# Rotary embedding moved from the retention blocks to the gate projection, and the last MLP's products reordered, in a two-block transformer kernel

## Chip, cores and metric

One core of a Trainium2 chip runs the whole program. The metric is the device time of one execution in microseconds: the kernel before has a median of 2659.2 us over 3 runs (2658.93 to 2669.19).

## What is computed

Two transformer blocks in float32, on 1024 tokens of 1024 features (cut to what the change touches):

```python
# block 1, token mixer: half of the width is retention, half gated linear attention (gla)
rq, rk, rv, rg, gq, gk, gv, gg, glr = split(u @ w_in)
q, k = rotary(rq), rotary(rk)          # [x1*cos - x2*sin, x2*cos + x1*sin] on each head of 128
ro = head_norm(retention(q, k, rv)) * silu(rg)
go = head_norm(gla(gq, gk, gv, log_a)) * silu(gg)
m  = concat(ro, go) @ w_out
# ... block 1's MLP, then block 2: mixer, cross attention, and at the end
h = layer_norm(ALPHA * h + relu(h @ w1)**2 @ w2)   # block 2's MLP: the output
```

## The kernel before

Every large product is made of three float32r matmuls (`mm3`, L114 to L116: high times high, high times low, low times high), so each operand is split into a high and a low page: ScalarE casts (L82), VectorE subtracts (L83). Pages of 128x1024 come from fixed pools: 8 each for W, H and X, 6 for S (staging), 6 of the smaller `half`. Loads are issued by SyncE in one queue. The program is written as Python generators that are woven; a scheduler with its own model then fixes one order of instructions for each engine, and each engine and each queue keeps to its order.

**The stretch around the rotary embedding.** `ret_proj` makes 24 tiles of 24 matmuls: first 8 token tiles of the gate `rg` (`tok_proj`: tanh on ScalarE, one VectorE product at L436, a store to DRAM), then 16 tiles of q and k by feature, which ScalarE copies out and stores in the DRAM tensor `r_qk`. For every 10 of these tiles about 3 steps of the 8 gla blocks are woven in (`gla_block`, three steps each; L544 are its score matmuls, L552 the VectorE copies that take them out of PSUM, L478 its last transposes). What is left of the gla blocks runs after the last tile. The gate's weights fill all 8 W pages; q and k are projected in four groups of 4 W pages. `ret_setup` loads the value weights `r_W` (8 W pages). Then 8 `ret_block`s follow in a pipe. Each loads its 128 columns of `r_qk` (L623), the same with the two halves of each head exchanged (L624, L625), and the cosines and sines (L626); GpSimd multiplies by the cosine (L631), VectorE by the sine (L632), VectorE adds (L633). In between TensorE projects the block's values (24 matmuls, L627). After L633 come the scores (L637) and the transposes of k (L642), the masking (L638, and L639 on GpSimd), the outputs (L648, L649), the state (L651, L654) and the head norm, which ends in transposes (L478, behind a GpSimd product, L475).

**The end.** `mlp` multiplies the hidden pages by the second weights in Strassen's form: seven half-size products, in groups of two over 8 chunks (`P[0]` in one half of PSUM, `P[1]` in the other), the last one, `T4`, alone:

```python
for g, prods in enumerate((((0, "B11"), (3, "T1")), ((4, "T2"), (5, "T3")), ((1, "B21"), (6, "B22")))):
    P = [banks(True), banks(False)]
...
P = banks(True)          # T4: rows 4 to 7
```

`T4` completes output tiles 4 to 7; tiles 0 to 3 are complete after the third group and are normalized and stored while `T4` runs. The last two chunks of `T4` are done tile by tile, so that each tile's normalization can start: subtract (L1023), statistics (L155), a chain of small VectorE instructions, the scaling (`normalize`: L171 on ScalarE for tiles below 4, else L173 on VectorE), the affine step (L1047, L1048) and the store.

Of the kernel before, what the change touches and what calls it, by code (L numbers as in the profile page):

```python
# [368 lines left out]
class Mix1(Net):  # L369
# [219 lines left out]

    def ret_proj(self, T):  # L590
        nc, I = self.nc, self.I
        self.r_gd = yield from self.tok_proj(T, 1536, "rg", True)
        self.r_qk = self.dram([128, 2, 4, S], "r_qk")
        for s in range(2):
            for g in range(2):
                W = self.wcols(I["w_in"], 512 * s + 256 * g, 256)
                for m in range(2):
                    for h in range(2):
                        ps = self.feat_out(T, W, slice(128 * m, 128 * m + 128), h)
                        o = self.ev()  # L600
                        nc.scalar.copy(out=o, in_=ps)
                        nc.scalar.dma_start(out=self.r_qk[:, s, 2 * g + m, 512 * h:512 * h + 512], in_=o)
                        yield

    def ret_setup(self):
        nc, I = self.nc, self.I
# [9 lines left out]
    def ret_block(self, i, T):  # L616
        nc = self.nc
        sl = slice(128 * i, 128 * i + 128)
        qk = self.page("H").rearrange("p (s h c) -> p s h c", s=2, c=128)
        sw = self.page("H").rearrange("p (s h c) -> p s h c", s=2, c=128)  # L620
        cs = self.half([128, 2, 128])
        vg = self.page("H")
        nc.sync.dma_start(out=qk, in_=self.r_qk[:, :, :, sl])  # L623
        nc.sync.dma_start(out=sw[0:64], in_=self.r_qk[64:128, :, :, sl])  # L624
        nc.sync.dma_start(out=sw[64:128], in_=self.r_qk[0:64, :, :, sl])  # L625
        nc.sync.dma_start(out=cs, in_=self.I["k_rot"][:, :, sl])  # L626
        nc.scalar.copy(out=vg[:, 0:512], in_=self.tok_out(T, self.r_W, i))  # L627
        nc.sync.dma_start(out=vg[:, 512:1024], in_=_rows(self.r_gd, i))
        v8 = lambda z: z.rearrange("p s h c -> p (s h) c")
        b8 = lambda z: cs[:, z].unsqueeze(1).broadcast_to([128, 8, 128])  # L630
        nc.gpsimd.tensor_tensor(out=v8(qk), in0=v8(qk), in1=b8(0), op=ALU.mult)  # L631
        nc.vector.tensor_tensor(out=v8(sw), in0=v8(sw), in1=b8(1), op=ALU.mult)  # L632
        nc.vector.tensor_tensor(out=qk, in0=qk, in1=sw, op=ALU.add)  # L633
        A, kT = sw[:, 0], sw[:, 1]
        ps = self.ps("tr").rearrange("p (h c) -> p h c", c=128)
        for h in range(4):
            nc.tensor.matmul(out=ps[:, h, :], lhsT=qk[:, 1, h, :], rhs=qk[:, 0, h, :], start=True, stop=True)  # L637
        nc.vector.tensor_tensor(out=A, in0=ps, in1=self.r_tab[:, 0], op=ALU.mult)  # L638
        nc.gpsimd.tensor_tensor(out=qk[:, 0], in0=qk[:, 0], in1=self.r_tab[:, 1], op=ALU.mult)  # L639
        ps = self.ps("tr").rearrange("p (h c) -> p h c", c=128)  # L640
        for h in range(4):
            nc.tensor.transpose(ps[:, h, :], qk[:, 1, h, :], self.ident)  # L642
# [13 lines left out]
        yield from self.head_norm(o[:, 0], vg[:, 512:1024], self.norm_w[:, 0:4], True, A, kT)  # L656
        nc.sync.dma_start(out=self.r_od[:, :, sl], in_=kT)
# [64 lines left out]
    def mlp(self, T, w1, w2, res, last, gate=None, then=None, end=None, aff=None):  # L722
# [249 lines left out]

        if gate is not None:
            gate = gate()
        for g, prods in enumerate((((0, "B11"), (3, "T1")), ((4, "T2"), (5, "T3")), ((1, "B21"), (6, "B22")))):
            P = [banks(True), banks(False)]
            for c in range(NC):
                if g == 0:
# [17 lines left out]
            for t in range(4):  # L996
                if g == 0:
                    nc.scalar.copy(out=R(t + 4), in_=P[1][t])
                elif g == 1:
                    tt(out=L(t + 4), in0=P[1][t], in1=R(t), op=ALU.add)  # L1000
                    tt(out=R(t), in0=R(t), in1=R(t + 4), op=ALU.add)
                    tt(out=R(t + 4), in0=R(t + 4), in1=L(t + 4), op=ALU.add)
                else:
                    tt(out=R(t), in0=P[1][t], in1=R(t), op=ALU.add)
        P = banks(True)
        tail = []
        for c in range(NC):
# [63 lines left out]
class Mix2(Mix1):  # L1071
# [714 lines left out]
    def block2_mlp(self, T):  # L1786
# [1 line left out]
        ln3 = self.affine(I["ln3_g_2"][0], I["ln3_b_2"][0])  # L1788

        def last(t, y, st):  # L1790
            self.normalize(y, y, t < 4, st)
            ln3(y)
            self.nc.sync.dma_start(out=_rows(self.O, t), in_=y)

# [145 lines left out]
```

## Time and profile before

| | |
|---|---|
| median of 3 runs | 2659.2 us |
| the profiled execution | 2663.38 us |
| its span, first to last instruction | 2661.6 us |
| mean granted TensorE clock | 0.978 |
| TensorE, VectorE busy | 2549.6 us (96%), 1886.3 us (71%) |
| ScalarE, GpSimd busy | 1170.3 us (44%), 240.3 us (9%) |

Around the span lie 1.8 us of the execution. Busy shares are means over stages with different limits; the stretch from 300 to 614 us (projections, gla and retention blocks) and the last 30 us are to be read by themselves.

### The profile page before, as it was taken

Reading aid. Unit: us, or ns where it says so; the run is one execution under the profiler, and the core shown is the slowest. Engines: PE = TensorE matmul, PEld = TensorE weight load, DVE = VectorE, ACT = ScalarE, POOL = GpSimd, SP = SyncE. Lnnn points to the kernel's source line nnn. Section 1 sums busy time; section 2 is a strip of 40 time slices with the busy share of each in tenths; the row PEclk is TensorE's granted clock in tenths of the full one; section 3 lists DMA queues with packets and bytes.
Section 4 is the critical chain, followed back from the end, with each engine's and each line's share of the span. In section 5 each row is a group of like instructions: output and inputs, shape, how many; then the busy total and the mean of one; then the engine's idle time right before and its main releaser. Section 6 shows DMA issues by size and latency. Waiting matters only on the chain. (4 is left out here: it accounts for less than half of the span.)

```text
span 2661.6 us, 33023 instructions
## 1 busy us (share of the span) xinstructions
PE 2549.6 (96%) x12086; PEld 2069.9 (78%) x12086; DVE 1886.3 (71%) x3205; ACT 1170.3 (44%) x1863; POOL 240.3 (9%) x222
## 2 busy tenths in 40 slices
PE   7899999889999999999999998999998999999997
PEld 7586777678888888888877776778876888888885
DVE  5858666688897777656965577785568777777759
ACT  3622233344654444433543574552237444444332
POOL 4121135540000000000000002100000000000000
PEclk8899999999999999999999999999998999999998
DMA  9772433464175668857632243361102755799763
GB/s 338 245 258 99 146 99 101 147 173 141 72 246 204 217 239 315 298 181 242 198 137 76 69 142 115 119 225 49 40 32 104 252 202 186 270 335 333 267 225 143
DMA packets 255130, 484.36 MB, mean 182 GB/s; under 512 B 21604, under 2 KB 110964, under 8 KB 254968
## 3 DMA queue, kind: packets, MB, share of 16 engines
q1 hardware_dynamic: 247768, 470.59, 51.4%
q10 hardware_dynamic: 7200, 11.67, 1.2%
q8 instruction: 95, 1.56, 0.2%
q14 instruction: 67, 0.55, 0.1%
HBM read 338.80 MB, written 143.38 MB: 181 GB/s over the span
## 5 line engine op out<-in xcount | busy, mean ns | idle before, releaser
L114 PE MATMUL ps<-U,W 128*128 128x512 f32 (+1 forms) x1080 | 427.4, 396 | 10.3 <-ACT ev L776 5.1
L114 PE MATMUL ps<-W,H 128*128 128x512 f32 x1088 | 425.2, 391 | 3.6 <-DVE sm L167 3.0
L83 DVE TENSOR_TENSOR W<-S,W 128x1024 fp32r<-128x1024 f32 (+1 forms) x272 | 333.4, 1229 | 132.5 <-ACT W L82 131.4
L115 PE MATMUL ps<-U,W 128*128 128x512 f32 (+1 forms) x1080 | 425.6, 394 | 1.5 <-DVE U L341 1.5
L115 PE MATMUL ps<-W,H 128*128 128x512 f32 x1088 | 424.5, 390 | 0.0
L116 PE MATMUL ps<-W,H 128*128 128x512 f32 x1088 | 424.4, 390 | 0.0
L116 PE MATMUL ps<-U,W 128*128 128x512 f32 (+1 forms) x1080 | 423.6, 392 | 0.8 <-DVE W L83 0.8
L82 ACT CAST W<-S 128x1024 fp32r<-128x1024 f32 x288 | 298.6, 1043 | 250.2 <-PE ps L115 167.9
L82 ACT CAST H<-S 128x1024 fp32r<-128x1024 f32 x130 | 136.5, 1050 | 292.0 <-PE ps L115 214.9
L83 DVE TENSOR_TENSOR H<-S,H 128x1024 fp32r<-128x1024 f32 x130 | 158.7, 1221 | 144.7 <-ACT H L82 139.9
L114 PEld LDWEIGHTS ps<-U,W 128*128 128x128 f32 (+1 forms) x1080 | 201.2, 186 | 60.7 <-ACT ev L776 5.4
L114 PEld LDWEIGHTS ps<-W,H 128*128 128x128 f32 x1088 | 204.8, 188 | 47.2 <-DVE X L1023 4.1
L115 PEld LDWEIGHTS ps<-U,W 128*128 128x128 f32 (+1 forms) x1080 | 201.3, 186 | 49.7 <-DVE U L341 4.6
L116 PEld LDWEIGHTS ps<-U,W 128*128 128x128 f32 (+1 forms) x1080 | 201.2, 186 | 46.6 <-DVE W L83 1.9
L116 PEld LDWEIGHTS ps<-W,H 128*128 128x128 f32 x1088 | 204.6, 188 | 42.2
L115 PEld LDWEIGHTS ps<-W,H 128*128 128x128 f32 x1088 | 204.8, 188 | 41.9
L116 PE MATMUL ps<-W,U 128*128 128x512 f32 x352 | 140.0, 398 | 5.4 <-DVE U L83 5.4
L114 PE MATMUL ps<-W,U 128*128 128x512 f32 x352 | 142.0, 403 | 1.2 <-DVE X L274 0.8
L115 PE MATMUL ps<-W,U 128*128 128x512 f32 x352 | 140.6, 399 | 0.4 <-DVE W L83 0.4
L776 ACT ACTIVATE ev<-ev 128x512 f32<-128x512 f32 x104 | 65.5, 630 | 140.0 <-DVE ev L874 116.6
L116 PEld LDWEIGHTS ps<-W,U 128*128 128x128 f32 x352 | 67.2, 191 | 20.6 <-DVE U L83 6.7
L777 ACT ACTIVATE X<-ev 128x512 f32<-128x512 f32 x128 | 81.0, 635 | 3.5
(527 smaller groups left out, 4521.2 us busy)
## 6 DMA issues: line engine op xcount, KB each, us to landing
S<-mlp_h SPq DMA_DIRECT2D x112, 512.0 KB, 5.0
S<-in_w_ff SPq DMA_DIRECT2D x96, 512.0 KB, 5.0
mlp_h<-X SPq DMA_DIRECT2D x96, 512.0 KB, 4.4
S<-in_mlp_w SPq DMA_DIRECT2D x96, 512.0 KB, 4.6
mlp_w<-S SPq DMA_DIRECT2D x96, 256.0 KB, 2.7
S<-mlp_w SPq DMA_DIRECT2D x48, 512.0 KB, 4.7
S<-in_w_in SPq DMA_DIRECT2D x46, 512.0 KB, 5.2
X<-in_w_ada SPq DMA_DIRECT2D x32, 512.0 KB, 6.7
```

The lines of the kernel that those rows point to most:

```text
L82: self.nc.scalar.copy(out=hi, in_=src)
L83: (lo_eng or self.nc.vector).tensor_tensor(out=lo, in0=src, in1=hi.bitcast(F32), op=ALU.subtract)
L114: mm(out=ps, lhsT=lh, rhs=rh, start=start and k == 0, stop=False)
L115: mm(out=ps, lhsT=lh, rhs=rl, start=False, stop=False)
L116: mm(out=ps, lhsT=ll, rhs=rh, start=False, stop=stop and k == n - 1)
L776: nc.scalar.activation(out=r, in_=x, func=ACTF.Relu)
L777: nc.scalar.activation(out=out, in_=r, func=ACTF.Square)
```

## The change

1. `ret_proj` projects q and k first, then the gate. After each gate tile it calls the new `rotate(i)`: the four loads of before, three VectorE products and sums (the cosine product too, which was GpSimd's), and a store of the result to a new DRAM tensor `r_rot`.
2. `ret_block` loads its columns from `r_rot`: one load in place of four, and no rotary arithmetic.
3. In the MLP of block 2 alone (`then is None`), `T4` runs third and the group of `B21` and `B22` last. So tiles 4 to 7 are completed early, and the tail, its last two chunks tile by tile, completes tiles 0 to 3 with two products each. `last` normalizes on ScalarE except for tile 3.

```diff
     def ret_proj(self, T):
         nc, I = self.nc, self.I
-        self.r_gd = yield from self.tok_proj(T, 1536, "rg", True)
         self.r_qk = self.dram([128, 2, 4, S], "r_qk")
+        self.r_rot = self.dram([128, 2, 4, S], "r_rot")
...
+        rg = self.tok_proj(T, 1536, "rg", True)
+        for i in range(NB):
+            next(rg)
+            self.rotate(i)
+            yield
...
+    def rotate(self, i):
...
+        nc.sync.dma_start(out=qk, in_=self.r_qk[:, :, :, sl])
+        nc.sync.dma_start(out=sw[0:64], in_=self.r_qk[64:128, :, :, sl])
+        nc.sync.dma_start(out=sw[64:128], in_=self.r_qk[0:64, :, :, sl])
+        nc.sync.dma_start(out=cs, in_=self.I["k_rot"][:, :, sl])
...
+        nc.vector.tensor_tensor(out=v8(qk), in0=v8(qk), in1=b8(0), op=ALU.mult)
+        nc.vector.tensor_tensor(out=v8(sw), in0=v8(sw), in1=b8(1), op=ALU.mult)
+        nc.vector.tensor_tensor(out=qk, in0=qk, in1=sw, op=ALU.add)
+        nc.sync.dma_start(out=self.r_rot[:, :, :, sl], in_=qk)
...
-        nc.sync.dma_start(out=qk, in_=self.r_qk[:, :, :, sl])
-        nc.sync.dma_start(out=sw[0:64], in_=self.r_qk[64:128, :, :, sl])
-        nc.sync.dma_start(out=sw[64:128], in_=self.r_qk[0:64, :, :, sl])
-        nc.sync.dma_start(out=cs, in_=self.I["k_rot"][:, :, sl])
+        nc.sync.dma_start(out=qk, in_=self.r_rot[:, :, :, sl])
...
-        nc.gpsimd.tensor_tensor(out=v8(qk), in0=v8(qk), in1=b8(0), op=ALU.mult)
-        nc.vector.tensor_tensor(out=v8(sw), in0=v8(sw), in1=b8(1), op=ALU.mult)
-        nc.vector.tensor_tensor(out=qk, in0=qk, in1=sw, op=ALU.add)
...
+        if then is None:
+
+            P = banks(True)
+            for c in range(NC):
+                (Hp, Wp), = operands(c, ((2, "T4"),))
+                product(P, c, Hp, Wp)
+                if c % 2:
+                    add_rest(4 + c // 2)
+            for t in range(4):
+                tt(out=L(t + 4), in0=L(t + 4), in1=P[t], op=ALU.subtract)
+            P = [banks(False), banks(True)]
+            tail = []
+            for c in range(NC):
+                ops = operands(c, groups[2])
+                if c >= NC - 2:
+                    tail.append((c, ops))
+                    continue
...
+                if c < 4:
+                    last(c + 4, y[c + 4], None)
+                    add_rest(c)
+            for t in range(4):
+                for c, ops in tail:
+                    for z, (Hp, Wp) in enumerate(ops):
+                        product(P[z], c, Hp, Wp, tiles=(t,))
+                tt(out=L(t), in0=P[0][t], in1=L(t), op=ALU.add)
+                tt(out=R(t), in0=P[1][t], in1=R(t), op=ALU.add)
+                last(t, y[t], None)
+            return
...
-            self.normalize(y, y, t < 4, st)
+            self.normalize(y, y, t != 3, st)
```

What this does to the order of two engines, at three places. Line numbers of the changed program are its own: L627 to L629 are the rotary instructions, L655 the scores of a retention block, L1096 and L1097 the affine step of the output (L1047 and L1048 before), L1050 and L1051 the last additions of the left and the right half of a tile.

VectorE where the value weights `r_W` are split (L83, W from S), before; the last gla blocks' copies out of PSUM (L549, L552) and factors (L536) stand around:

```order
L536 TENSOR_TENSOR X_4033<-X_4023,H_4020 128x896
L536 TENSOR_TENSOR X_4072<-X_4062,H_4020 128x896
L83 TENSOR_TENSOR W_4259<-S_4257,W_4258 128x1024
L83 TENSOR_TENSOR W_4265<-S_4263,W_4264 128x1024
L549 TENSOR_TENSOR half_3875<-ps_3889,ident 128x256
L552 COPY_PREDICATED half_3875<-half_2298,ps_3889 128x256 x3
L552 COPY_PREDICATED half_3875<-half_2298,ps_3902 128x256 x2
L83 TENSOR_TENSOR X_4273<-S_4271,X_4272 128x1024
L552 COPY_PREDICATED half_3875<-half_2298,ps_3902 128x256
```

The same place in the changed program (sm and rs are the small instructions of gla block 4's head norm):

```order
L627 TENSOR_TENSOR H_3948<-H_3948,half_3950 128x1024
L461 SCALAR_TENSOR_TENSOR sm_3812<-sm_3812,sm_3803 128x4
L629 TENSOR_TENSOR H_3908<-H_3908,H_3909 128x1024
L135 TENSOR_SCALAR sm_3815<-sm_3812 128x4
L628 TENSOR_TENSOR H_3949<-H_3949,half_3950 128x1024
L143 TENSOR_TENSOR rs_3816<-sm_3815 128x4
L559 TENSOR_SCALAR sm_4044<-H_3695 128x2
L629 TENSOR_TENSOR H_3948<-H_3948,H_3949 128x1024
L144 TENSOR_TENSOR rs_3816<-rs_3816,sm_3812 128x4
L83 TENSOR_TENSOR W_4342<-S_4340,W_4341 128x1024
L145 SCALAR_TENSOR_TENSOR rs_3816<-rs_3816 128x4
L83 TENSOR_TENSOR W_4348<-S_4346,W_4347 128x1024
```

In the changed program the second page of `r_W` (the row W_4342) stands behind the rotary instructions of the last token tiles; before, no such row was there.

TensorE where the last tile of the projection ends and the first value tiles begin, before (ps_3842 is the last q and k tile, ps_4307 the first value tile, L544 gla block 6):

```order
L116 MATMUL ps_3842<-U_615,W_3607 128x512
L544 MATMUL ps_3889<-H_3873 128x128 x2
L544 MATMUL ps_3889<-X_3886,X_3876 128x128 x6
L544 MATMUL ps_3902<-X_3886,X_3876 128x128 x8
L573 MATMUL ps_3969<-ident,H_3954 128x128 x2
L114 MATMUL ps_4307<-W_4246,U_613 128x512
L544 MATMUL ps_3928<-H_3873 128x128 x2
L544 MATMUL ps_3928<-X_3925,X_3915 128x128 x6
L578 MATMUL ps_3973<-H_3639,H_3954 128x256
```

And in the changed program (ps_4392 and ps_4439 are the first two value tiles):

```order
L114 MATMUL ps_4392<-W_4341,U_613 128x512
L114 MATMUL ps_4439<-W_4335,U_613 128x512
L115 MATMUL ps_4439<-W_4336,U_613 128x512
L116 MATMUL ps_4439<-W_4335,U_614 128x512
L114 MATMUL ps_4439<-W_4335,U_613 128x512
L115 MATMUL ps_4439<-W_4336,U_613 128x512
L116 MATMUL ps_4439<-W_4335,U_614 128x512
L114 MATMUL ps_4439<-W_4341,U_613 128x512
L115 MATMUL ps_4392<-W_4342,U_613 128x512
```

In the changed program two value tiles start before gla blocks 6 and 7, and the row that reads W_4342 waits for the VectorE row of that name above; TensorE has two value tiles fewer to fill the gaps of the blocks behind.

VectorE at the end of the program, before (X_19671 is the last tile, X_19668 the one ahead of it):

```order
L1048 TENSOR_TENSOR X_19665<-X_19665,bc_21025 128x1024
L173 TENSOR_SCALAR X_19668<-X_19668,sm_21341,sm_21345 128x1024
L1023 TENSOR_TENSOR X_19671<-X_19671,ps_20930 128x512
L1047 TENSOR_TENSOR X_19668<-X_19668,bc_21023 128x1024
L155 BN_STATS st_20847<-X_19671 128x6
L1048 TENSOR_TENSOR X_19668<-X_19668,bc_21025 128x1024
```

And in the changed program (X_19703 is the last tile, X_19700 the one ahead, X_19697 the one ahead of that):

```order
L1097 TENSOR_TENSOR X_19697<-X_19697,bc_20755 128x1024
L1050 TENSOR_TENSOR X_19703<-ps_20661,X_19703 128x512
L1096 TENSOR_TENSOR X_19700<-X_19700,bc_20753 128x1024
L1051 TENSOR_TENSOR X_19703<-ps_20663,X_19703 128x512
L1097 TENSOR_TENSOR X_19700<-X_19700,bc_20755 128x1024
L155 BN_STATS st_21404<-X_19703 128x6 x2
```

The last tile now has two additions and two halves of statistics where it had one of each, and its TensorE work is twice as long.

## Rows read from the trace of the kernel before

**Rows 1.** The page, busy time of the engines, share of the span, instructions.

```profile
PE 2549.6 (96%) x12086; PEld 2069.9 (78%) x12086; DVE 1886.3 (71%) x3205; ACT 1170.3 (44%) x1863; POOL 240.3 (9%) x222
```

**Rows 2.** Timeline of TensorE: start, us, engine, line, operation [idle before it].

```profile
415.67 0.49 PE L544 MATMUL ps<-H 64*128 64x128 f32 x4
...
524.42 0.66 PE L478 MATMUL ps<-ident,H 128*128 128x128 f32 x4 [1.86 <-POOL H L475]
...
613.94 0.66 PE L478 MATMUL ps<-ident,H 128*128 128x128 f32 x4 [0.71 <-POOL H L475]
```

**Rows 3.** Busy time by stretch: length, engines (instructions), granted clock, DMA share, GB/s.

```profile
300.00:404.60 104.60, 94.21 (x582) 77.44 (x582) 66.33 (x160) 32.26 (x60) 34.86 (x53) 0.95 0.33 114
404.60:524.40 119.80, 102.78 (x642) 83.61 (x640) 76.76 (x196) 44.21 (x91) 67.75 (x68) 0.96 0.39 124
524.40:613.90 89.50, 80.34 (x487) 69.40 (x487) 73.58 (x200) 42.08 (x112) 36.90 (x22) 0.96 0.65 175
...
2635.00:2661.60 26.60, 9.47 (x33) 6.81 (x31) 22.20 (x52) 0.00 (x0) 0.00 (x0) 0.72 0.24 99
```

**Rows 4.** Waits of TensorE in 404.6 to 524.4: total, times, longest.

```profile
PE ps L544 <- DVE half L552: 12.0, 4, 7.1
```

**Rows 5.** Waits of TensorE in 524.4 to 613.9.

```profile
PE ps L637 <- DVE H L633: 4.5, 3, 2.1
PE ps L478 <- POOL H L475: 4.0, 4, 1.9
```

**Rows 6.** Instructions of L632 over the run: min/median/max ns.

```profile
L632 DVE TENSOR_TENSOR H<-H,half x8: 1211/1226/1799, 516.5 to 594.5; 128x1024 f32<-128x1024 f32 x8
```

**Rows 7.** Instructions of L436 over the run.

```profile
L436 DVE SCALAR_TENSOR_TENSOR ev<-ev,ps x16: 631/684/689, 234.8 to 343.5; 128x512 f32<-128x512 f32 x16
```

**Rows 8.** Groups in 404.6 to 524.4, VectorE: count, busy, mean ns, idle before.

```profile
L83 DVE TENSOR_TENSOR W<-S,W 128x1024 fp32r<-128x1024 f32 x6 | 10.9, 1849 | 4.8 <-ACT W L82 4.8
```

**Rows 9.** Groups in 524.4 to 613.9, GpSimd.

```profile
L631 POOL TENSOR_TENSOR H<-H,half 128x1024 f32<-128x1024 f32 x6 | 14.3, 2386 | 10.9 <-DMA H<-r_qk 7.7 <-issue 3.2
L475 POOL TENSOR_TENSOR H<-H,H 128x512 f32<-128x512 f32 x8 | 12.4, 1549 | 16.7 <-ACT H L469 14.1 <-DVE st L155 2.6
```

**Rows 10.** Timeline of VectorE, then GpSimd, at 543.

```profile
543.23 2.31 DVE L135 TENSOR_SCALAR sm<-sm 128x4 int32<-128x4 int32 x1
545.58 0.16 DVE L143 TENSOR_TENSOR rs<-sm 128x4 f32<-128x4 f32 x1
...
543.12 2.40 POOL L631 TENSOR_TENSOR H<-H,half 128x1024 f32<-128x1024 f32 x1
```

**Rows 11.** DMA of L623: issue in ns min/median/max, and landing.

```profile
L623 SPq DMA_DIRECT2D H<-r_qk x8: 518/526/566, 500.8 to 587.3; - x8
...
DMA to landing us min/median/max: 4.1/4.6/5.3
```

**Rows 12.** Timeline of TensorE at the end, its last matmul the last row.

```profile
2643.07 0.50 PE L114 MATMUL ps<-W,H 128*128 128x512 f32 x1 [3.04 <-DVE sm L167]
...
2644.61 0.63 PE L115 MATMUL ps<-W,H 128*128 128x512 f32 x1
2645.04 0.63 PE L116 MATMUL ps<-W,H 128*128 128x512 f32 x1
...
2647.05 0.39 PE L115 MATMUL ps<-W,H 128*128 128x512 f32 x1
2647.28 0.40 PE L116 MATMUL ps<-W,H 128*128 128x512 f32 x1
```

**Rows 13.** Groups in 2600 to 2661.6, VectorE.

```profile
L1047 DVE TENSOR_TENSOR X<-X,bc 128x1024 f32<-128x1024 f32 x8 | 9.8, 1220 | 0.2 <-ACT X L171 0.2
L155 DVE BATCH_NORM_STATS2 st<-X 128x6 f32<-128x512 f32 x12 | 8.1, 685 | 0.0
...
L1023 DVE TENSOR_TENSOR X<-X,ps 128x512 f32<-128x512 f32 x4 | 2.7, 670 | 0.0
```

**Rows 14.** Timeline of VectorE, its last instruction.

```profile
2656.68 1.23 DVE L1048 TENSOR_TENSOR X<-X,bc 128x1024 f32<-128x1024 f32 x1
```

More of the change, by code (lines that the diff above doesn't have):

```diff
@@ L603, in ret_proj @@
                         yield
+        rg = self.tok_proj(T, 1536, "rg", True)
[3 more added lines that the diff above has]
+            yield
+        try:
+            next(rg)
+        except StopIteration as e:
+            self.r_gd = e.value
+    def rotate(self, i):
+        nc = self.nc
+        sl = slice(128 * i, 128 * i + 128)
+        qk = self.page("H").rearrange("p (s h c) -> p s h c", s=2, c=128)
+        sw = self.page("H").rearrange("p (s h c) -> p s h c", s=2, c=128)
+        cs = self.half([128, 2, 128])
+        nc.sync.dma_start(out=qk, in_=self.r_qk[:, :, :, sl])
+        nc.sync.dma_start(out=sw[0:64], in_=self.r_qk[64:128, :, :, sl])
+        nc.sync.dma_start(out=sw[64:128], in_=self.r_qk[0:64, :, :, sl])
+        nc.sync.dma_start(out=cs, in_=self.I["k_rot"][:, :, sl])
+        v8 = lambda z: z.rearrange("p s h c -> p (s h) c")
+        b8 = lambda z: cs[:, z].unsqueeze(1).broadcast_to([128, 8, 128])
+        nc.vector.tensor_tensor(out=v8(qk), in0=v8(qk), in1=b8(0), op=ALU.mult)
+        nc.vector.tensor_tensor(out=v8(sw), in0=v8(sw), in1=b8(1), op=ALU.mult)
+        nc.vector.tensor_tensor(out=qk, in0=qk, in1=sw, op=ALU.add)
+        nc.sync.dma_start(out=self.r_rot[:, :, :, sl], in_=qk)
     def ret_setup(self):
@@ L620, in ret_block @@
         sw = self.page("H").rearrange("p (s h c) -> p s h c", s=2, c=128)
-        cs = self.half([128, 2, 128])
         vg = self.page("H")
-        nc.sync.dma_start(out=qk, in_=self.r_qk[:, :, :, sl])
-        nc.sync.dma_start(out=sw[0:64], in_=self.r_qk[64:128, :, :, sl])
-        nc.sync.dma_start(out=sw[64:128], in_=self.r_qk[0:64, :, :, sl])
-        nc.sync.dma_start(out=cs, in_=self.I["k_rot"][:, :, sl])
+        nc.sync.dma_start(out=qk, in_=self.r_rot[:, :, :, sl])
         nc.scalar.copy(out=vg[:, 0:512], in_=self.tok_out(T, self.r_W, i))
         nc.sync.dma_start(out=vg[:, 512:1024], in_=_rows(self.r_gd, i))
-        v8 = lambda z: z.rearrange("p s h c -> p (s h) c")
-        b8 = lambda z: cs[:, z].unsqueeze(1).broadcast_to([128, 8, 128])
-        nc.gpsimd.tensor_tensor(out=v8(qk), in0=v8(qk), in1=b8(0), op=ALU.mult)
-        nc.vector.tensor_tensor(out=v8(sw), in0=v8(sw), in1=b8(1), op=ALU.mult)
-        nc.vector.tensor_tensor(out=qk, in0=qk, in1=sw, op=ALU.add)
         A, kT = sw[:, 0], sw[:, 1]
@@ L974, in mlp @@
             gate = gate()
-        for g, prods in enumerate((((0, "B11"), (3, "T1")), ((4, "T2"), (5, "T3")), ((1, "B21"), (6, "B22")))):
+        groups = (((0, "B11"), (3, "T1")), ((4, "T2"), (5, "T3")), ((1, "B21"), (6, "B22")))
+        for g, prods in enumerate(groups if then is not None else groups[:2]):
             P = [banks(True), banks(False)]
@@ L1004, in mlp @@
                     tt(out=R(t), in0=P[1][t], in1=R(t), op=ALU.add)
+        if then is None:
[15 more added lines that the diff above has]
+                for z, (Hp, Wp) in enumerate(ops):
+                    product(P[z], c, Hp, Wp)
+                if c < 4:
[3 more added lines that the diff above has]
+                for c, ops in tail:
+                    for z, (Hp, Wp) in enumerate(ops):
+                        product(P[z], c, Hp, Wp, tiles=(t,))
[3 more added lines that the diff above has]
+            return
         P = banks(True)
```

## The prediction

> **What bounds the kernel now.** I read the page's busy times first: TensorE is busy 96% of the span, VectorE 71% [rows 1]. As a mean this says that moving VectorE work is worth nothing except where TensorE stands still, so the next view is the busy time by stretch, cut at three TensorE instructions [rows 2, 3]: from the 17th tile of the old projection (48 products of 0.2265 us ahead of the L544 at 415.67, so 404.6) to gla's last transposes at 524.4, and on to retention's last transposes at 613.9. In the stretch ahead, 300 to 404.6, TensorE is idle for 10.4 of 104.6 us; in the first of the two for 17.0 of 119.8; in the second for 9.2 of 89.5. Those are the places where the rotary embedding is made or will be made. The waits say who is late: in the first stretch the copies out of PSUM at L552, 12.0 us in four waits [rows 4]; in the second the rotary sum L633, 4.5 us, and GpSimd's product L475, 4.0 us, which is nearly all of the 9.2 [rows 5]. At the program's end VectorE is the busier: 22.2 of 26.6 us against TensorE's 9.5 [rows 3].
>
> The sum is made against the profiled execution, 2663.4 us, which lies 4.2 us above the median of 2659.2; I subtract that at the end. About 0.5%, 13.3 us, is what a measurement of this kernel can tell from no change.
>
> **a. Ahead of the old seventeenth tile (300 to 404.6).** The gate's 8 products of 0.684 us [rows 7] go later, 5.5 us of VectorE work. TensorE's 10.4 us of idle there can shrink by some of it, but gla's copies, its cause, stay. I take -1 us; bounds -4 (most of the 5.5) and +1 (the order of the gla steps against the tiles changes too).
>
> **b. The gate stretch (119.8 us before).** The last 8 projection tiles are now the gate's, and each is followed by `rotate`. Added on VectorE: 24 operations of 128x1024. L632 is such an operation, 1.226 us [rows 6]: 29.4 us. The gate's products add 5.5, and two rotary steps that lay in this stretch leave, some 2.4. VectorE's need goes from 76.8 [rows 3] to 76.8 + 29.4 + 5.5 - 2.4 = 109.3 us of 119.8, or 91%. TensorE's own need, 102.8, is no larger. Two things decide whether VectorE at 91% delays TensorE. First, VectorE's order is fixed. The rotary operations wait for loads; one of L623 took 4.6 us from issue to landing [rows 11], and each needs four loads, then gives a store, 40 transfers on SyncE's queue of 0.53 us each to issue, 21 us; block 5's loads for gla stand behind some. Whatever copy out of PSUM is queued behind a rotary operation waits too, and TensorE waits for it. Second, the value weights. Before, four of the eight W pages came free between the groups of q and k, so that half of `r_W` was split early; now the gate holds all eight until its last tile. The split of the second page (W_4342) stands behind the last rotary operations on VectorE, while on TensorE the product that reads it stands ahead of gla blocks 6 and 7 (both orders above). From the gate's last tile VectorE has about two token tiles' rotary work (6 x 1.226 = 7.4 us) and a split of 1.85 [rows 8] to finish: some 9 us of wait, of which the products of the first page on two value tiles cover about 2. I take 7 for it, 3 for the copies held up behind the first load and its store, and another 3 for the copies L552 that wait already and now queue behind a 91% busy engine. So +13 us. Bounds: 0, if VectorE finds all of it in its own gaps (109.3 is below 119.8); and +28, if each of the 24 rotary operations takes 1.85 us, as L83's on the same size do in this stretch [rows 8] (then VectorE's need is 124.3), with L552's 12.0 us doubled and partly overlapping that. I take a value in the middle because the nearest row, L632, was measured at 1.226 as its median, but beside little GpSimd work, and the stretch has 67.8 us of it [rows 3].
>
> **c. The retention blocks (89.5 us before).** Each block loses three loads, the multiplication on GpSimd (L631, 2.39 us, 6 of the 8 in this stretch [rows 9]) and two VectorE operations (2 x 1.226, for six or seven blocks some 16 us of 73.6). The path from load to scores was: landing 4.6, L631 2.4 with L632 beside it, L633 1.2; now only a landing. So the wait for L633, 4.5 us, goes, and I take two thirds of the one for L475, 4.0 us [rows 5], because GpSimd is freed of 14.3 us. The rest of the head norm's chain is on ScalarE and VectorE and stays. Two value tiles' products were started in stretch b, 19 matmuls of 0.2265, 4.3 us less. That is -4.5 -2.7 -4.3 = -11.5; against it stands a new wait at the start, where three blocks' first loads, masks and norms meet at once: half a microsecond net. I take -11; bounds -5 (the first wait is replaced by another, as scores, masks and norm follow each other inside a block anyway, and only the matmuls done earlier count) and -15 (all the idle time of 9.2, and 4.3, and a steadier clock: the granted clock here is 0.96 [rows 3], which is worth some 2 us).
>
> GpSimd gives one thing more. L135, an instruction on four columns, took 2.31 us at 543.23, from the start of an L631 of 2.40 us to its end, where the next small one took 0.16 [rows 10]: VectorE stood still while GpSimd read. There is a rule for this in the Trainium skill, "SBUF — State Buffer", section "SBUF: two separate sides": the port pair that GpSimd and VectorE share is a lock that one instruction holds to its end, and a VectorE operation with two SBUF inputs needs it against a GpSimd operation that reads SBUF. The trace agrees, with the 2.31 us above. The rule speaks for stretch c, where L631 goes, and against stretch b, where all 24 new operations have two SBUF inputs: by it the sum there would lie at the upper bound instead of in the middle.
>
> **d. The end.** Before, TensorE waits 3.04 us at 2643.07, put down to VectorE [rows 12]: with one product per tile it is at half of a PSUM tile whose other half VectorE is still reading. Behind that wait its matmuls start 0.43 us apart (2644.61, 2645.04) and at the end 0.23 (2647.05, 2647.28) [rows 12], at a granted clock of 0.72 [rows 3]: ten or so of them cost 0.2 us too much, 2 us. Now each of the four tiles has two products, 24 matmuls, 5.4 us, and TensorE doesn't run into VectorE: counted in the changed order with the durations of [rows 13], the last group holds about 42 us of VectorE work on 43 us of TensorE's. So TensorE ends 5.2 us earlier, with as many products as before. What follows it becomes longer. Before, from the last matmul's end, 2647.28 + 0.40 [rows 12], to the last instruction's, 2656.68 + 1.23 [rows 14], there are 10.2 us. The last tile now has a second addition (0.670, as L1023) and a second statistics instruction (0.685) [rows 13], 1.35 us. And VectorE's work per tile is 2 x 0.67 + 2 x 0.685 + 1.9 for the chain of small instructions + 2 x 1.22 = 7.1 us against TensorE's 5.4, so it falls behind, by what its free time doesn't make up: I take 0.9. The net is -5.2 + 2.3 = -2.9, so -3; bounds -6 (no backlog, and the scaling on ScalarE relieves it) and +1 (TensorE waits once for a PSUM tile, and the three tiles' backlog of 1.7 each stands at the end).
>
> **Sum.** -1 + 13 - 11 - 3 = -2: 2661.4 us for the profiled kind of execution, 2657 for the median.
>
> **The rivals.**
>
> *VectorE absorbs it (faster).* Its need of 109.3 us fits into 119.8, and TensorE waits for neither the rotary results (they are needed a stretch later) nor, if the loads come early, for the value weights. Then b is 0 and the other terms stay: -1 + 0 - 12 - 3 = -16, or 2643. For it: TensorE's idle time is already in the stretch, and the rotary work may fall into the same gaps. Against: L552 is already late by 12.0 us with VectorE at 64%.
>
> *VectorE piles up at the gate's end (slower).* GpSimd's work meets the 24 rotary operations, which take 1.85 us each; VectorE's need, 124.3, passes the stretch's own 119.8. From that point each further microsecond of VectorE is one of TensorE, in front of the second page of the value weights above all. Then b is +28, c gives only -8 since the first retention blocks start with VectorE behind, and d -3: -1 + 28 - 8 - 3 = +16, or 2675. For it: L83's mean of 1.849 us [rows 8]; against: rotary operations have slack of their own, and L632 had a maximum of 1.8 but a median of 1.226 [rows 6]. It is also the case that the rule in the Trainium skill, "SBUF — State Buffer", section "SBUF: two separate sides", would give, as GpSimd's reads would hold the rotary operations up.
>
> *The change's gain is hidden anyway (no change).* TensorE's 80.3 of 89.5 us in the retention blocks is its own, and when L633 is no longer late the next link is: the masks or the head norm. c is -5, and with b at +9: -1 + 9 - 5 - 3 = 0, or 2659.
>
> **How the numbers follow.** The forecast has a chance of 0.48, the last rival, which lies beside it, 0.12, the faster one 0.25 and the slower one 0.15. Hence faster by over 0.5% (below 2645.9) 0.25, within 0.5% 0.60, slower (above 2672.5) 0.15. The range takes in the faster case down to c's lower bound, 2640, and goes up to 2673, short of the slower case's middle; that leaves out some 0.05 below and 0.13 above.
>
> **What would show it right or wrong.** Right: VectorE near 90% busy between the first gate tile and gla's last transposes, and that stretch about 133 us long; TensorE's longest waits there for L83's pages of `r_W` and for L552; the retention stretch about 78 us, with no wait for a rotary sum; at the end no wait of 3 us on TensorE, and 12 to 13 us of VectorE behind its last matmul. Wrong: rotary operations well above 1.3 us on average, or a gate stretch not longer than 120 us, or the scores waiting for the new load, which would put a landing of 4.6 us where L633 was.

## The result, and the profile after

The changed kernel takes 2682.5 us (median of 6 runs, 2677.8 to 2684.7), the kernel before 2665.9 in the same comparison (2658.9 to 2669.2, 6 runs): a ratio of 1.0069, 95% interval 1.0059 to 1.0079, by which it is 18 us slower. The forecast was no change, with 2640 to 2673. The profiled execution has a span of 2680.9 us.

The busy time by stretch, cut at the same three places as [rows 3] (start of the last eight projection tiles, gla's last transposes, retention's last transposes); columns are length, then TensorE, its weight loads, VectorE, ScalarE, GpSimd with instructions, granted clock, DMA share, GB/s:

```profile
300.00:409.30 109.30, 100.53 (x618) 82.17 (x617) 62.46 (x162) 29.44 (x56) 27.44 (x37) 0.97 0.32 106
409.30:563.50 154.20, 113.92 (x632) 88.27 (x631) 105.07 (x228) 46.80 (x95) 71.26 (x82) 0.87 0.60 170
563.50:641.13 77.63, 73.06 (x469) 64.87 (x468) 47.84 (x187) 42.33 (x112) 20.23 (x16) 0.98 0.55 167
```

The gate stretch grew from 119.8 to 154.2 us, 34.4; the retention stretch shrank from 89.5 to 77.6, 11.9. The start came 4.7 us later and the rest of the program was 7.9 shorter, of which the experiments below give 3 to 6 to the end. How far two executions of one order differ can be read from the kernel before and the one with the last products alone (below): every engine has the same order in both up to the last MLP, yet gla's last transposes lie at 524.4 and 529.5 us, and the retention blocks end at 613.9 and 620.3. So differences of up to some 6 us between two traces can be scatter. In the gate stretch TensorE's idle time rose from 17.0 to 40.3 us, and its busy time from 102.8 to 113.9 although it ran 10 matmuls fewer: the granted clock fell from 0.96 to 0.87. VectorE is busy for 105.1 of 154.2 us, 68%, not the forecast 91%.

Waits of TensorE in that stretch (total, times, longest):

```profile
PE ps L544 <- POOL X L537: 9.5, 5, 5.2
PE ps L115 <- DVE W L83: 8.1, 1, 8.1
PE ps L544 <- DVE rs L144: 5.7, 1, 5.7
PE ps L573 <- POOL H L564: 4.7, 3, 2.3
PE ps L544 <- DVE half L552: 4.5, 5, 2.2
PE ps L567 <- DVE half L552: 4.0, 5, 2.8
```

The wait for the value weights, 8.1 us, was foreseen. The others are of gla's matmuls, and no one of them is large: they wait for GpSimd's products (L537, L564) and for VectorE's copies. Before, one kind, the 12.0 us of [rows 4], was most of the 17.0 us of idle time.

TensorE's rows (start, us) at three of those places, a product after the first of them, and gla's last transposes:

```profile
496.81 0.79 PE L115 MATMUL ps<-W,U 128*128 128x512 f32 x1 [8.07 <-DVE W L83]
...
502.02 0.63 PE L115 MATMUL ps<-W,U 128*128 128x512 f32 x1
...
513.34 3.22 PE L544 MATMUL ps<-X,X 64*128 64x128 f32 x28 [5.19 <-POOL X L537]
...
542.60 2.08 PE L544 MATMUL ps<-X,X 64*128 64x128 f32 x16 [5.71 <-DVE rs L144]
...
563.47 0.63 PE L478 MATMUL ps<-ident,H 128*128 128x128 f32 x4
```

The gate's tiles are finished at 481, as TensorE ran through them without a gap from 440 to 461, and what can be made of the value tiles without their second page at 489. From 508 to 555 it has little but the last gla blocks, and waits again and again. After the wait of 8.07 us its products take 0.63 us each in place of 0.39: the lower clock. Three pieces of the stretch, with the columns of above:

```profile
440.00:461.00 21.00, 21.00 (x94) 17.31 (x93) 14.98 (x36) 3.54 (x8) 3.69 (x2) 1.00 0.89 256
488.00:508.00 20.00, 11.34 (x43) 7.77 (x41) 12.68 (x24) 5.06 (x14) 8.05 (x11) 0.74 0.80 243
508.00:555.00 47.00, 26.32 (x178) 21.27 (x178) 34.60 (x76) 14.23 (x25) 29.68 (x31) 0.75 0.22 70
```

The granted clock was 1.00 where TensorE was busy throughout, and 0.74 and 0.75 where it was busy for 11.3 of 20 and 26.3 of 47 us.

How late gla's loads are is seen on SyncE. The loads of the last gla blocks' q, k and decay (L523), before:

```profile
375.23 0.54 SPq L523 DMA_DIRECT2D H<-g_qkb  x1
404.59 0.53 SPq L523 DMA_DIRECT2D H<-g_qkb  x1
433.60 0.52 SPq L523 DMA_DIRECT2D H<-g_qkb  x1
465.24 1.89 SPq L523 DMA_DIRECT2D H<-g_qkb  x1
```

and after, the same four blocks, with the rotary step's first load (L621):

```profile
406.79 0.52 SPq L621 DMA_DIRECT2D H<-r_qk  x1
...
409.88 0.54 SPq L523 DMA_DIRECT2D H<-g_qkb  x1
...
457.67 0.54 SPq L523 DMA_DIRECT2D H<-g_qkb  x1
...
496.26 0.61 SPq L523 DMA_DIRECT2D H<-g_qkb  x1
...
501.10 0.57 SPq L523 DMA_DIRECT2D H<-g_qkb  x1
```

Before, a gla block's load follows the one before it by 29 to 32 us. Now the first of the four comes 35 us late, right behind the first rotary loads, which have to wait for all of q and k; the others come 53, 63 and 36 us late.

The rotary operations themselves, VectorE's groups in 409 to 563.5:

```profile
L627 DVE TENSOR_TENSOR H<-H,half 128x1024 f32<-128x1024 f32 x8 | 10.6, 1323 | 2.8 <-DMA H<-r_qk 2.6 <-DMA half<-in_k_rot 0.2
L629 DVE TENSOR_TENSOR H<-H,H 128x1024 f32<-128x1024 f32 x8 | 9.7, 1218 | 0.1
L628 DVE TENSOR_TENSOR H<-H,half 128x1024 f32<-128x1024 f32 x8 | 9.7, 1211 | 1.3 <-DMA H<-r_qk 1.3
```

They took 30.0 us in all, as forecast (29.4). One of the 24 met a GpSimd product, L537 from 475.49 to 477.60, and took longer:

```profile
476.62 2.05 DVE L627 TENSOR_TENSOR H<-H,half 128x1024 f32<-128x1024 f32 x1
```

The other 23 took 1.19 to 1.23 us each.

### The profile page after: what moved, and what is told of

It reads as the page before. It is cut to its first block, busy times and chain, and to the rows that moved or that the text cites. A ratio compares the mean times of both kernels' runs of the same rounds, so it can differ in the third digit from the quotient of the medians.

```text
span 2680.9 us, 33034 instructions
## 1 busy us (share of the span) xinstructions
PE 2551.6 (95%) x12086; PEld 2069.3 (77%) x12086; DVE 1877.9 (70%) x3213; ACT 1172.6 (44%) x1866; POOL 218.5 (8%) x214
## 5 line engine op out<-in xcount | busy, mean ns | idle before, releaser
L114 PE MATMUL ps<-U,W 128*128 128x512 f32 (+1 forms) x1080 | 428.2, 397 | 10.2 <-ACT ev L794 5.1
L83 DVE TENSOR_TENSOR W<-S,W 128x1024 fp32r<-128x1024 f32 (+1 forms) x272 | 330.7, 1219 | 137.7 <-ACT W L82 136.9
L83 DVE TENSOR_TENSOR H<-S,H 128x1024 fp32r<-128x1024 f32 x130 | 158.6, 1220 | 144.3 <-ACT H L82 139.8
L115 PEld LDWEIGHTS ps<-W,U 128*128 128x128 f32 x352 | 67.4, 192 | 23.6 <-DVE W L83 9.9
L116 PEld LDWEIGHTS ps<-W,U 128*128 128x128 f32 x352 | 67.4, 191 | 20.1 <-DVE U L83 6.3
```

The source lines that it names most:

```text
L83: (lo_eng or self.nc.vector).tensor_tensor(out=lo, in0=src, in1=hi.bitcast(F32), op=ALU.subtract)
L114: mm(out=ps, lhsT=lh, rhs=rh, start=start and k == 0, stop=False)
L115: mm(out=ps, lhsT=lh, rhs=rl, start=False, stop=False)
L116: mm(out=ps, lhsT=ll, rhs=rh, start=False, stop=stop and k == n - 1)
```

## The experiments

Theory H: the rotary step's two H pages per tile, of a pool of eight that gla uses too, hold back gla's loads. Theory V: the 24 operations' time on VectorE. Theory W: the gate last holds all W pages, so that value weights come late. A fourth, SyncE's order, came up with them. In the table the two middle columns are the times at which the last transposes of gla and of retention start, in the one profiled execution (so up to some 6 us between two rows can be scatter); each ratio is against the kernel before on the same chip, with intervals of about 0.0013 to either side.

| kernel | gla | retention | ratio |
|---|---|---|---|
| before | 524.4 | 613.9 | 1 |
| whole change | 563.5 | 641.1 | 1.0069 |
| last products alone | 529.5 | 620.3 | 0.9989 |
| rotary step alone | 562.0 | 639.6 | 1.0098 |
| swapped order alone | 531.0 | 630.4 | 1.0051 |
| rotary step, no arithmetic | 548.6 | 624.6 | 1.0033 |
| rotary step, X pages | 554.4 | 631.8 | 1.0055 |
| rotary step, ScalarE's queue | 581.8 | 657.6 | 1.0139 |
| rotary step, gate first | 566.8 | 646.1 | 1.0108 |
| rotary step, gate first, X pages | 541.6 | 634.7 | 1.0078 |
| no arithmetic, free products | 564.1 | 640.0 | 1.0080 |
| no arithmetic, tied products | 560.9 | 636.6 | 1.0060 |
| rotary step, broadcast pages | 554.5 | 630.6 | 1.0045 |
| last products, a gla page from S | 537.1 | 634.0 | 1.0031 |
| whole change, a gla page from S | 544.7 | 622.6 | 1.0000 |
| the same, rotary X pages | 559.6 | 635.4 | 1.0046 |
| the same, rotary broadcast pages | 557.3 | 634.0 | 1.0045 |

**The last MLP's products alone.** Its edit is the diff's hunks in `mlp` and `last`, without the others.

> Only the reordered products of the last MLP, the rotary embedding as before. The traces differ by -7.9 us behind the retention blocks, so all theories expect about -8 us against before (ratio 0.997); my forecast's own term for the end was -3 (0.999). A ratio above 1.000 would mean that the end's gain in the changed kernel came from somewhere else.

Measured: 0.9989 (0.9980 to 0.9998), 2659.4 against 2662.0 us: 2.9 us faster (0.0011 of 2662). That is the forecast's term, and not the 7.9 us of the two traces. The interval reaches from 0.5 to 5.3 us. All kept traces together say a little more: from retention's last transposes to the end, the eleven with the old last MLP take 2042.2 to 2047.7 us (mean 2044.5), the six with the new one 2036.0 to 2040.5 (mean 2038.7), 5.8 less. TensorE's and then VectorE's last rows:

```profile
2645.88 0.39 PE L115 MATMUL ps<-W,H 128*128 128x512 f32 x1
2646.11 0.39 PE L116 MATMUL ps<-W,H 128*128 128x512 f32 x1
```

```profile
2655.80 1.23 DVE L1079 TENSOR_TENSOR X<-X,bc 128x1024 f32<-128x1024 f32 x1
```

There is no TensorE wait left in the last 60 us, where [rows 12] has 3.04. From the last matmul's end, 2646.50, to VectorE's, 2657.03, there are 10.5 us, against 10.2 before. VectorE hardly fell behind.

**The rotary step alone.** The diff without its hunks in `mlp` and `last`.

> Only the moved rotary embedding, the last MLP as before. All theories: +27 us against before (ratio 1.010), the gate stretch about 154 us, the retention stretch about 78. The sum with the kernel of the last MLP's products alone should be the whole change's +19 us; if not, the two parts act on each other.

Measured: 1.0098 (1.0084 to 1.0111), 26 us. All of the loss, and more, is the rotary step's; the two parts add up to 23 us against the whole's 18, which the intervals hardly tell apart. Where nothing else is said, the kernels that follow start from this one.

**The swapped order alone.** From the kernel before, with the rotary embedding in the retention blocks:

```diff
     def ret_proj(self, T):
-        self.r_gd = yield from self.tok_proj(T, 1536, "rg", True)
         self.r_qk = self.dram([128, 2, 4, S], "r_qk")
...
+        self.r_gd = yield from self.tok_proj(T, 1536, "rg", True)
```

> Only the projections' order is changed (q and k first, then the gate); the rotary embedding stays in the retention blocks. Theory W (the gate last holds all eight W pages, the value weights come late and TensorE lacks their products as filling): most of the loss is here, +15 us or more (1.006). Theory H (the rotary step's two H pages and its loads in SyncE's queue hold back the loads of the gla blocks) and theory V (VectorE's 24 added operations): within 5 us of before (0.998 to 1.002), gla loads about 29 us apart as before.

Measured: 1.0051 (1.0039 to 1.0063), 13.6 us. Stretches cut as before, then SyncE's loads of gla:

```profile
404.00:530.96 126.96, 105.42 (x648) 83.39 (x646) 85.04 (x204) 43.89 (x90) 68.53 (x68) 0.96 0.39 116
530.96:630.39 99.43, 84.22 (x492) 73.05 (x493) 76.23 (x201) 42.31 (x112) 36.81 (x22) 0.93 0.61 160
```

```profile
374.81 0.55 SPq L523 DMA_DIRECT2D H<-g_qkb  x1
403.75 0.53 SPq L523 DMA_DIRECT2D H<-g_qkb  x1
432.98 0.53 SPq L523 DMA_DIRECT2D H<-g_qkb  x1
```

The swap doesn't delay gla's loads. Gla ends 6.6 us later than in the kernel before, but only 1.5 later than with the last products alone, whose order there is the old one. The clear part is in the retention stretch, 99.4 us against 89.5, where the waits for the rotary sum L633 rose from the 4.5 of [rows 5] to 9.4 us; that part can't be in the changed kernel, where L633 is gone from the blocks. The wait that theory W names is small: TensorE waits for the value weights' L83 for 1.8 us here, and not for 8.1. So the swap costs time, but the way of theory W isn't shown.

**Loads and store without arithmetic.** The three `nc.vector.tensor_tensor` lines of `rotate` are left out, and with them the rotary embedding.

> The moved rotary step keeps its pages, its loads and its store, but its 24 VectorE operations are left out (so the rotary embedding itself is left out); last MLP as before. Theory V: the loss goes, the gate stretch falls to about 120 us and the whole to about -10 us against before (0.996), since the retention blocks keep their gain. Theory H: the loss stays, +15 us or more (1.006), gla loads still 40 us and more apart. Theory W: about +15 too, with a wait for the value weights of several us, but gla loads 30 us apart.

Measured: 1.0033 (1.0020 to 1.0046), between the theories.

```profile
409.31 0.54 SPq L523 DMA_DIRECT2D H<-g_qkb  x1
449.97 0.52 SPq L523 DMA_DIRECT2D H<-g_qkb  x1
479.69 0.53 SPq L523 DMA_DIRECT2D H<-g_qkb  x1
```

With no arithmetic at all gla's loads still come 34 to 46 us late, and gla ends 17.6 us later than with the swap alone (548.6 against 531.0). The arithmetic adds another 13.4 (562.0). So more than half of the delay of gla's end is there without any of the work that the forecast had counted on VectorE.

**Other pages and other queues.** In `rotate`, `self.page("X")` for `self.page("H")`; or `nc.scalar.dma_start` for `nc.sync.dma_start`, five times.

> The moved rotary embedding alone, with its two pages per tile taken from the X pool in place of the H pool; everything else as in the kernel with only the moved rotary step (+26 us, 1.0098). Theory H (pages): the gla loads come 30 us apart again, gla's last transposes move from 562 to about 544 us and the whole falls to about +8 us (1.003), as the difference between the kernel without the arithmetic and the one with only the swap was 18 us at that point. Theory V (VectorE's time): nothing changes, +22 us or more.

> The moved rotary embedding alone, with its four loads and its store issued on ScalarE's queue in place of SyncE's; pages from H. If SyncE's fixed order (gla's loads queued behind rotary loads and stores) is the cause: gla loads about 30 us apart, +8 us (1.003). If the pages themselves are (theory H in the narrow sense): gla loads still 40 us apart, +20 us or more (1.0075). A new cost is possible: ScalarE issues them, and whatever waits there stands ahead of its exponentials.

Measured: 1.0055 (1.0043 to 1.0067) with X pages, 1.0139 (1.0124 to 1.0154) with ScalarE's queue. Gla's loads with X pages:

```profile
377.38 0.55 SPq L523 DMA_DIRECT2D H<-g_qkb  x1
401.45 0.53 SPq L523 DMA_DIRECT2D H<-g_qkb  x1
482.57 0.67 SPq L523 DMA_DIRECT2D H<-g_qkb  x1
```

and with ScalarE's queue, H pages:

```profile
409.72 0.58 SPq L523 DMA_DIRECT2D H<-g_qkb  x1
472.88 0.58 SPq L523 DMA_DIRECT2D H<-g_qkb  x1
521.55 0.58 SPq L523 DMA_DIRECT2D H<-g_qkb  x1
```

SyncE carries no rotary transfer in the second kernel, and gla's loads are as late as ever, so rotary transfers in its queue aren't needed for the delay. This kernel doesn't rule out the order of the queue, though. SyncE's own waits from 410 to 522 us in it:

```profile
SPq L439 <- DVE ev L436: 52.0, 6, 18.4
SPq L523 <- DMA r_rot<-H: 10.7, 2, 6.3
```

Gla's loads wait for rotary pages to be stored, 10.7 us, but SyncE spends far more on the gate's stores (L439), which stand between gla's loads in its order. What speaks for the pages is the first kernel: with pages from X and the same queue two loads are on time. The third is not; it stands behind rotary loads in the queue. Gla's end gains 7.6 us of the 31 that separate the rotary step from the swap. So theory H holds for the first two loads, but that they are on time doesn't give gla's pace back.

**The gate first.** `ret_proj` in the old order, then eight steps `self.rotate(i); yield`, with H and with X pages.

> The order of the projections as before (gate first, then q and k), and the moved rotary step as eight steps of its own behind them, pages from H, loads on SyncE's queue. Theory W (the swap's own share, +13.6 us measured): about +12 us (1.0045), with no wait of 8 us for the value weights. Theory H or V alone: as with the swap, +20 us or more, since the same 24 operations and 16 pages now stand in the shorter stretch that is left for gla.

> As the one before (gate first), with the rotary step's pages from X. If pages and order are the whole cause, the retention stretch's gain of 12 us is left against a few us of VectorE: -5 to +2 us (0.998 to 1.001). If VectorE's 29 us of arithmetic costs by itself, +8 us or more (1.003).

Measured: 1.0108 (1.0094 to 1.0123) and 1.0078 (1.0066 to 1.0091), 29 and 21 us. Both came out on the side of theories H and V, +20 and +8 us or more, and against W: undoing the swap isn't a gain when the rotary step then stands in the shorter rest of the stretch. With X pages gla ends at 541.6, and the retention stretch takes 93.0 us, until 634.7, so this run doesn't show that VectorE's time alone is the price.

**Products that nothing reads.** To the kernel without arithmetic, three products per tile are added on a page of their own. First free, then behind a copy from the loaded tile:

```diff
+        nc.vector.tensor_copy(out=self.r_pad[:, 0:1], in_=sw[:, 0, 0, 0:1])
+        for _ in range(3):
+            nc.vector.tensor_tensor(out=self.r_pad, in0=self.r_pad, in1=self.r_pad, op=ALU.mult)
```

> As the kernel without the rotary arithmetic (its loads and store stay, the rotary embedding is left out), but with 24 VectorE products of the same size on a page of their own that nothing reads. If VectorE's time by itself is the price of the arithmetic: back to about +26 us against before (1.0098). If the price is that the arithmetic keeps the two H pages of a tile longer: stays near the kernel without arithmetic, +9 us (1.0033). Half and half would be +17 (1.0065).

> As the kernel without the rotary arithmetic (the rotary embedding is left out), with three VectorE products per token tile on a page of their own, now tied to their place: a copy of one column of the loaded tile stands ahead of them. The free products of the kernel before this one were drawn forward to 310 to 366 us and cost 15 us there, so that run said nothing about the gate stretch. VectorE's time in the gate stretch as the price of the arithmetic: gla's last transposes back at about 562 us, +26 us (1.0098). The hold on the pages as the price: about 549 us, +9 us (1.0033).

Measured: 1.0080 (1.0066 to 1.0094) free, 1.0060 (1.0047 to 1.0072) tied. The free ones were drawn forward, into 314 to 366 us, as this row of VectorE shows:

```profile
326.75 9.34 DVE L630 TENSOR_TENSOR bc<-bc 128x1024 f32<-128x1024 f32 x6
```

Gla's transposes that start at 366.74 without the products start at 382.05 with them, and an offset of 15.4 us is still there at retention's end (640.0 against 624.6): the placement, not the gate stretch, was measured. The tied products lie in the gate stretch, whose time was:

```profile
406.00:560.92 154.92, 117.62 (x630) 91.00 (x629) 113.24 (x236) 45.98 (x95) 75.22 (x82) 0.86 0.62 172
```

Gla ends at 560.9, 12.3 us later than without products; 10.8 of it once the 1.5 us that this execution was already late at 366.7 are taken off. By that, VectorE's time is most of the arithmetic's 13.4 us at that point; by the ratios it is 0.0027 of 0.0065, some 40%. So two fifths to four fifths, and with intervals of 0.0013 on each ratio and some 6 us of scatter between traces even that is rough. That the rest is the longer hold on the pages is likely, and not shown.

**Pages away from gla.** The rotary step's pages from the pool of three broadcast pages; then, from the other side, one gla page from the staging pool, `qkb = self.page("S")` in `gla_block`, with the last products alone and with the whole change.

> The moved rotary step alone, with its pages from the pool of three broadcast pages, which neither gla nor a weight uses in this stretch; arithmetic, loads and queue as in the kernel with only the moved rotary step (+26 us). Theory H: the gla loads come 30 us apart, gla's last transposes lie below 545 us, the whole at +10 us or less (1.004). Theory V: +20 us or more (1.0075). With three pages the rotary tiles come one at a time, so the gate's page of the output product, which is from the same pool, may be late; TensorE doesn't need it in this stretch.

> The last MLP's new order alone (0.9989), and one of the three H pages of a gla block taken from the staging pool S, rotary embedding as before. If the pace of gla, a block in 29 us, is set by the H pages already in the kernel before, the gla loads come closer together and the whole falls to -10 us or lower (0.996). If it is set by the block's own chain of engines, the pace stays at 29 us and the ratio at 0.999.

> The whole change, and one of the three H pages of a gla block from S. Theory H: most of the pages' share of the loss goes, the gla loads come 30 us apart, +18 us becomes +5 us or less (1.002). Theory V: +13 us or more stays (1.005).

Measured: 1.0045 (1.0032 to 1.0058), 1.0031 (1.0019 to 1.0043) and 1.0000 (0.9991 to 1.0009). With broadcast pages the last four loads come at 378.56, 406.98, 449.68 and 486.56, and gla ends at 554.5, as with X pages: between the theories. In the old order gla's pace was not set by the pages: with one page from S that kernel is slower, which neither branch had forecast. In the changed kernel the same one-line edit takes away 18 us, all of the loss. Gla's loads don't come 30 us apart in it; three come at once, all four 29 to 112 us earlier than in the whole change:

```profile
380.67 4.25 SPq L523 DMA_DIRECT2D S<-g_qkb  x3
...
421.00 1.82 SPq L523 DMA_DIRECT2D S<-g_qkb  x1
```

Its retention stretch:

```profile
544.66:622.63 77.97, 73.93 (x474) 65.66 (x473) 47.79 (x187) 42.45 (x112) 20.31 (x16) 0.98 0.56 166
```

It is as short as in the whole change; the gain is ahead of it, at gla's end, 544.7 in place of 563.5.

**Both sides relieved.** The whole change, a gla page from S, and the rotary pages from X or from the broadcast pages.

> The whole change with both sides relieved: one gla page from S (which alone brought the whole change from 1.0069 to 1.0000) and the two rotary pages from X. If the pages still cost something there: -5 us or lower against before (0.998). If what is left is VectorE's time and the swap, no change from 1.0000.

> The same with the rotary pages from the three broadcast pages. If pages are what is left: -5 us or lower (0.998), with gla loads about 30 us apart. If it is VectorE's time and the swap: 1.0000 as with one gla page from S alone. The rotary tiles come one at a time here, which could make the last of them late for the first retention block.

Measured: 1.0046 (1.0033 to 1.0060) and 1.0045 (1.0033 to 1.0058). Both missed, 12 us slower than with the gla page alone. Gla's loads in the first of them:

```profile
385.66 4.04 SPq L523 DMA_DIRECT2D S<-g_qkb  x3
...
410.46 0.52 SPq L523 DMA_DIRECT2D S<-g_qkb  x1
```

They are as early as with the gla page alone, and yet gla ends at 559.6 in place of 544.7. Each edit also gives another order of the program, and what in these orders costs the 12 us stays open. It bears on the run before: of the 18 us that the gla page gave back, these runs can't say how much is the pages and how much the order that came with them.

## Why the prediction was wrong

**Step a**, -1 us: the stretch ahead ended 4.7 us later in the profiled execution (409.3 against 404.6). In the kernel with the rotary step alone, which has the same order there, the gate's first product starts at 404.83. A term of 1 us can't be told from that scatter.

**Step b**, +13 us with bounds 0 and +28, is the step that failed: it measured 34.4. Two of its parts were right, the rotary operations' number and time (30.0 us against 29.4) and the wait for the value weights (8.1 us against 7). Wrong was the measure itself, VectorE's capacity: 109.3 us of work in 119.8 of room. VectorE was busy for 68% of the stretch that came of it, and the kernel without any rotary arithmetic, for which this measure gives no loss, still ended gla at 548.6, 24 us later than before (19 later than with the last products alone).

What the runs show in its place are two terms. TensorE's idle time grew by 23.3 us: the wait of 8.1 us is in it, and many short ones of gla's matmuls, for blocks whose loads came 35, 53, 63 and 36 us late. "Block 5's loads for gla stand behind some" is in the text, and was priced at 3 us, together with the copies. The other 11.1 us are slow clock, 0.87 against 0.96: in the pieces with the waits TensorE was granted 0.74 and 0.75, and its products there took longer, so these waits were paid for twice. I had left the clock out of b altogether. The gate's tiles, which had filled TensorE's gaps between gla blocks, were used up at 481 us, and the last three blocks had little beside them.

Why the loads are late is shown in part. Pages of a pool are given out in the program's order, so gla's next pages come free behind rotary pages which wait for the last of q and k; with the rotary pages from X or from the broadcast pool the first two loads are on time. How much of the loss is due to it isn't settled. From the swap alone to the rotary step alone gla's end moves by 31.0 us in single traces: 17.6 with loads, pages and stores, 13.4 with the arithmetic. Other rotary pages give back 7.5 of it, a gla page from S 18.8 in the whole change; but with loads as early as in that kernel the two kernels relieved on both sides give back only 3.9 and 6.2. The order of the program, which every one of these edits changes, is a rival that no run here holds still.

**Step c**, -11 us: measured -11.9 (77.6 against 89.5), with no wait for a rotary sum. The size was right partly by luck. TensorE's idle time fell from 9.2 to 4.6 us, where the terms for it gave 6.7 less; the matmuls done earlier were 18, some 4.1 us; the other 3.2 are shorter products, at a granted clock of 0.98 against 0.96, which stood in the bound alone.

**Step d**, -3 us: measured -2.9 by the ratio of 0.9989, and -5.8 by the means of all traces. Of its parts, TensorE's gain of 5.2 us is borne out: there is no wait of 3 us any more, and the last products start 0.23 us apart, where ten of them stood 0.43 apart [rows 12]. What VectorE has left behind TensorE was priced too high: it grew by 0.3 us and not by 2.3.

**The rivals.** The slower one named 2675 us or +16, and +18 was measured. Its place, the end of the gate stretch, was right; its mechanism was not, so the number came near by luck. The rotary operations took 1.21 to 1.32 us on average, not 1.85. By the rule of the Trainium skill, "SBUF — State Buffer", section "SBUF: two separate sides", they could be held up wherever GpSimd's 71.3 us of work ran at the same time. The trace agrees for the one that did, with 2.05 us. The other 23 found GpSimd idle; between 405 and 500 us it waited for gla's loads (21.4 us), for the output weights (16.8) and for ScalarE (21.4). The rule's effect is in the trace at another place too (last section). The faster rival fell with b; its sum has -12 for c where "the other terms stay" would give -11. The third, a hidden gain, fell too: c came in full.

**The range** failed because the upper bound of b was a bound on one resource, and a chain of waits isn't bounded by the busy time of one engine in it. The two terms named for the bound don't give it either: 124.3 us is 4.5 over 119.8, and L552's waits once more are 12.0, 16.5 in all and not 28.

## What to carry to other kernels

When a step is moved to where an engine has room, look first at what else the stretch hands around: pages of a pool that another loop draws from in a fixed order, and the spacing of that loop's loads. An engine's free share says little where a chain of blocks leaves TensorE waiting: here more than half of the delay of gla's end came without the added arithmetic, and the waits cost clock as well. Take a control that keeps the transfers and leaves the arithmetic out, and a second trace of one order, to know the scatter. One line (here a gla page from another pool) can undo such a loss, but each edit also changes the fixed order, and two that were to help further cost 12 us here. The best version measured is still the last products' new order without the rotary move, 0.9989.

## What was unexpected in the hardware's behaviour

GpSimd's hold on VectorE showed up on gla's own operations. VectorE's L536 and GpSimd's product for the output weights (L690) in the changed kernel, one engine to a fence:

```profile
507.49 1.17 DVE L536 TENSOR_TENSOR X<-X,H 128x896 f32<-128x896 f32 x1 [7.29 <-ACT X L534]
...
513.32 3.23 DVE L536 TENSOR_TENSOR X<-X,H 128x896 f32<-128x896 f32 x1 [4.13 <-POOL X L537]
```

```profile
513.25 2.35 POOL L690 TENSOR_TENSOR S<-S,bc 128x1024 f32<-128x1024 f32 x1
```

The second L536 took 3.23 us, 2.3 of them until L690 ended; the other seven took 1.08 to 1.46 us, and 1.08 to 1.09 where GpSimd did nothing beside them. Work for the output weights, which the first output products read at about 635 us, thus stood in front of gla's chain. And 29 us of VectorE products that nothing reads, drawn ahead into 314 to 366 us, went with gla's transposes 15.3 us later there, although VectorE is only some 60% busy in that part of the kernel before (66.3 of 104.6 us).
